# Two-layer hybrid decoder on one core: other dates for the modulation rows, other engines for the first squares

## The chip, the cores and the metric

The kernel runs on one core of one Trainium2 chip. The metric is the time of one execution on the device in microseconds (us); of several executions the median is given. Lower is better. A core has TensorE (matrix products into PSUM), VectorE, ScalarE, GpSimd, and SyncE, which here issues the transfers from HBM into SBUF. The profile calls them PE (PEld for TensorE's weight loads), DVE, ACT, POOL and SP.

## The reference

256 tokens of width 1024 pass through two layers. Each layer is a half-step SwiGLU feed-forward, a token mixer, and a second half-step feed-forward. The mixer of layer 0 is stick-breaking attention, that of layer 1 a gated linear recurrence (RG-LRU). Every sub-layer is normalised and modulated by shift, scale and gate, which come from one conditioning vector c:

```python
c_act = jax.nn.silu(c)
for layer in range(DEPTH):
    mod = (c_act @ mod_w[layer] + mod_b[layer]).reshape(B, N_SUB, 3, D_MODEL)
    h, g = sublayer_input(x, norm_g[layer, 0], mod[:, 0])     # rmsnorm(x) * (1 + scale) + shift, 1 + gate
    x = x + MACARON_W * g * swiglu(h, ffn_w_gu[layer, 0], ffn_w_down[layer, 0])
    h, g = sublayer_input(x, norm_g[layer, 1], mod[:, 1])
    y = stick_breaking_attention(...) if layer == 0 else rglru_block(...)
    x = x + g * y
    h, g = sublayer_input(x, norm_g[layer, 2], mod[:, 2])
    x = x + MACARON_W * g * swiglu(h, ffn_w_gu[layer, 1], ffn_w_down[layer, 1])
return rmsnorm(x, final_norm_g)
```

All is float32. The modulation weights are 2 x 9 x 1024 rows of 1024 numbers, and each layer's 9 x 1024 results are needed before the sub-layer that uses them.

## The kernel before

**Stages.** Six stages follow each other: feed-forward (0, 0), attention, feed-forward (0, 2), feed-forward (1, 0), the recurrent layer, feed-forward (1, 2). Counted as stages they are the first to the sixth; feed-forward (0, 2) is the third and (1, 0) the fourth. The activations x stay in SBUF for the whole program, transposed, as 8 chunks of 128 x 256.

**Products.** To get float32 accuracy from a faster product, each weight block `raw` is split into a high part `wh` (ScalarE, line 520) and a rest `wl` (VectorE, line 523); activations are split the same way into `hx` or `arenar` pairs. One group (line 549) is three products of 128 x 128 by 128 x 256: wh with the high part, wh with the rest, wl with the high part. A feed-forward has an up phase, 22 tiles of 8 x 2 groups that are followed by silu and a multiply, and a down phase of 8 x 22 groups, at the end of each eighth of which a residual is added to x (line 719). In a few places a product is done in plain float32 instead (lines 567, 1151).

**Start of a stage.** The next stage's first up tiles use x times the scale alone (`scaled`, lines 642 to 644; 258 columns, the two more carry the shift). Meanwhile the sums of squares are added over the partitions by a product with ones (line 626), ScalarE turns them into 1/rms (`rms`, `rst`, by Ln and Exp), and `norm_chunk` writes the 8 normalised chunks: a multiply on VectorE (line 652, `hpre`), a split on ScalarE (`hx`) and VectorE (line 656). `hk` is a second copy of one chunk. In the recurrent layer follow the convolutions (lines 1130 and 1133, VectorE), the gates (line 1151, TensorE), and later decays, scans and outputs (lines 1208 to 1224), which the first float32 product of its down phase (line 567) waits for.

**Modulation rows.** A row, in this text, is one block of 128 x 1024 modulation weights, 0.5 MB, which a transfer brings into one of three `rawm` buffers; VectorE multiplies it by silu(c) and sums along it in one instruction (line 582, with a short second record for reading the sum). There are 143 of these, and one row, the first scale row, goes in two halves (line 842). The first 16 belong to the first normalisation: `first_scale` and `early` load them one by one between the first weights. The other 128 are in a list, `todo`. A function made by `hook` is called at every up tile and at every block of the down phase, with a position from 0 to 42; it adds `rate` per step to an account and takes a row off the list for every whole one. At positions from a given one on it takes all that are still missing up to `due`.

**Order of the work.** Nothing is issued in the order in which it is written. Every operation is recorded with an estimated cost, and a list scheduler (`Program.schedule`) puts each engine's instructions into a fixed order, by due times that come from TensorE's order and by the buffers that are free. The estimates (`LAT0`, `RATE`, `c_mm`) are the scheduler's alone: they change the order, and no instruction. At run time each engine, and SP's queue of transfers, works through its list in order and waits at the head. A transfer into a buffer that is still in use holds up all transfers behind it.

**The start.** ScalarE loads the first parameters; SP loads c, x in two halves, two modulation rows, then the first weights. Silu of c, spread over the partitions by TensorE (line 1282), is `cact`, in two halves. The squares of x's chunks are split over ScalarE and VectorE (`square`, line 1290) and added on VectorE (line 1293) into one sum for each half of x. TensorE sums both over the partitions and does eight products that nobody reads (line 1274). Then comes the first normalised chunk, and with it the first real products, 16 in float32 (line 567, `bank<-sg,raw`).

## Time and profile before

| | |
|---|---|
| median of 3 runs | 964.79 us (963.89 to 965.85) |
| the profiled execution, its own time | 967.32 us |
| its span, first to last instruction | 965.6 us |
| granted TensorE clock, mean over the span | 0.998 |
| moved by DMA | 251.25 MB, 260 GB/s over the span |
| DMA engines' busy share, queue of SP | 70.3% |

How to read the profile: times are us from the first instruction. A row of the timeline has start, duration, engine, line of the code, operation, output<-input by the program's names, shapes, and in brackets the idle time ahead with what ended it. A record of TensorE includes the way through its pipeline, so that consecutive products overlap; their pace is read from the starts. A row of the windows has, after the stretch and its length, the busy time of PE, PEld, DVE, ACT and POOL with the number of instructions, the clock, the DMA engines' share and GB/s. With one line picked out, only that line's engine is shown. In the view of waits stand the total, the number of times and the longest.

### The profile page before, as it was taken

To read this page: it belongs to the slowest core of one execution; us is meant where nothing else is said; L and a number is where in the kernel's file an instruction comes from. 1 tells how busy PE (TensorE), PEld (TensorE's weight loads), DVE (VectorE), ACT (ScalarE), POOL (GpSimd) and SP (SyncE) were. 2 spreads that over 40 slices of the span, in tenths; PEclk is the share of its full clock that TensorE was granted. 3 is DMA by queue.
4 is the path that set the end of the run, shared out by engine and by line. 5 is a ranking of instruction groups with operands and counts; after the bars stand their busy time and mean duration, and the time that the engine had idled before them with its cause. 6 is when DMAs were issued, how large, how long until landed. Compare 5 with 4: busy or idle time off the path is not lost.

```text
span 965.6 us, 19759 instructions
## 1 busy us (share of the span) xinstructions
PE 949.1 (98%) x8090; PEld 935.7 (97%) x8090; DVE 799.3 (83%) x1343; ACT 575.6 (60%) x935; POOL 3.8 (0%) x16
## 2 busy tenths in 40 slices
PE   7999999999999999999999999999999999999996
PEld 5999999999999999999999999999899999999996
DVE  6889979999999998888999877799997996555551
ACT  5666555559886765554456444544679785444441
POOL 0000000000000000000000000000000000000000
PEclk9999999999999999999999999999999999999999
DMA  8988989965766599788986877799643746555521
GB/s 296 373 298 319 356 302 344 343 254 212 249 235 207 188 331 359 278 300 299 357 326 238 302 267 292 278 340 349 246 162 134 262 162 238 210 176 209 185 88 44
DMA packets 49341, 251.25 MB, mean 260 GB/s; under 512 B 5601, under 2 KB 6497, under 8 KB 30434
## 3 DMA queue, kind: packets, MB, share of 16 engines
q1 hardware_dynamic: 48530, 249.30, 70.3%
q8 instruction: 63, 1.03, 0.4%
q10 hardware_dynamic: 720, 0.69, 0.2%
q14 instruction: 28, 0.23, 0.1%
HBM read 248.92 MB, written 1.05 MB: 259 GB/s over the span
## 4 chain that ended last, share of the span: by engine, by line
PE 83%; DVE 8%; DMA 5%; ACT 2%; issue 1%; SPq 0%; DVEq 0%; ACTq 0%
PE bank L549 77%; DMA rawm<-in_modw 3%; PE bank L954 2%; DVE wl L523 2%; PE bank L567 1%; DVE rawm L582 1%; DVE arenaf L1133 1%; DMA raw<-in_win 1%; PE bank L1077 1%; ACT arenaf L499 1%; PE bank L1030 1%; PE bank L1055 1%; DMA x<-in_xT 1%; DVE hpre L652 0%; ACT wh L520 0%
## 5 line engine op out<-in xcount | busy, mean ns | idle before, releaser
L549 PE MATMUL bank<-hx,wh 128*128 128x256 f32 (+1 forms) x3204 | 556.7, 278 | 0.4 <-DVE hx L656 0.2
L520 ACT ACTIVATE wh<-raw 128x1024 fp32r<-128x1024 f32 (+1 forms) x332 | 340.7, 1033 | 278.1 <-PE bank L549 172.4
L549 PEld LDWEIGHTS bank<-hx,wh 128*128 128x128 f32 x3204 | 486.7, 188 | 2.0 <-DVE hx L656 0.9
L523 DVE TENSOR_TENSOR wl<-raw,wh 128x1024 fp32r<-128x1024 f32 (+1 forms) x332 | 391.7, 1189 | 103.4 <-ACT wh L520 102.5
L549 PE MATMUL bank<-hx,wl 128*128 128x256 f32 (+1 forms) x1602 | 444.3, 277 | 0.0
L549 PEld LDWEIGHTS bank<-hx,wl 128*128 128x128 f32 x1602 | 301.3, 188 | 0.0
L549 PE MATMUL bank<-arenar,wh 128*128 128x256 f32 x1664 | 284.4, 277 | 0.0
L549 PEld LDWEIGHTS bank<-arenar,wh 128*128 128x128 f32 x1664 | 251.0, 188 | 0.1
L549 PE MATMUL bank<-arenar,wl 128*128 128x256 f32 x832 | 229.7, 276 | 0.0
L582 DVE SCALAR_TENSOR_TENSOR rawm<-rawm,cact 128x1024 f32<-128x1024 f32 x143 | 173.9, 1219 | 17.3 <-DMA rawm<-in_modw 16.9
L549 PEld LDWEIGHTS bank<-arenar,wl 128*128 128x128 f32 x832 | 156.2, 188 | 0.0
L499 ACT ACTIVATE arenar<-a 128x256 fp32r<-128x256 f32 x88 | 35.4, 404 | 3.7 <-DVE a L797 2.4
L719 DVE SCALAR_TENSOR_TENSOR x<-bank,mf,x 128x256 f32<-128x256 f32 x48 | 22.6, 478 | 17.3 <-PE bank L549 17.3
L802 DVE TENSOR_TENSOR arenar<-a,arenar 128x256 fp32r<-128x256 f32 x88 | 36.5, 418 | 0.0
L549 PE MATMUL bank<-hk,wh 128*128 128x256 f32 x156 | 31.1, 290 | 0.5 <-ACT hk L499 0.5
L792 DVE TENSOR_TENSOR a<-bank,sg 128x256 f32<-128x256 f32 x74 | 30.7, 417 | 0.3 <-ACT sg L499 0.3
L499 ACT ACTIVATE hx<-x,mf 128x256 fp32r<-128x256 f32 x40 | 19.7, 504 | 18.7 <-DVE x L719 18.3
L499 ACT ACTIVATE hx<-hpre,mf 128x256 fp32r<-128x256 f32 x48 | 23.5, 502 | 10.9 <-DVE hpre L652 10.8
L499 ACT ACTIVATE sg<-bank 128x256 f32<-128x256 f32 x74 | 27.1, 369 | 3.8 <-PE bank L549 2.9
L499 ACT ACTIVATE sq<-x 128x256 f32<-128x256 f32 x45 | 17.8, 403 | 15.6 <-DVE x L719 15.6
L549 PEld LDWEIGHTS bank<-hk,wh 128*128 128x128 f32 x156 | 24.0, 188 | 1.1 <-ACT hk L499 0.7
L499 ACT ACTIVATE arenaf<-bank 128x384 f32<-128x384 f32 (+1 forms) x45 | 21.4, 525 | 4.8 <-PE bank L1030 1.6
(120 smaller groups left out, 588.4 us busy)
## 6 DMA issues: line engine op xcount, KB each, us to landing
rawm<-in_modw SPq DMA_DIRECT2D x144, 512.0 KB, 6.1
raw<-in_gu SPq DMA_DIRECT2D x72, 1024.0 KB, 5.3
raw<-in_wdn SPq DMA_DIRECT2D x44, 1024.0 KB, 4.8
raw<-in_win SPq DMA_DIRECT2D x10, 1024.0 KB, 7.5
raw<-in_qk SPq DMA_DIRECT2D x8, 1024.0 KB, 6.3
raw<-in_gu SPq DMA_DIRECT2D x13, 512.0 KB, 6.9
raw<-in_gu SPq DMA_DIRECT2D x7, 768.0 KB, 4.2
raw<-in_wout SPq DMA_DIRECT2D x5, 1024.0 KB, 4.9
```

Source lines behind the costliest of these rows:

```text
L499: act.activation(o(), i(), f, **{k: (v() if callable(v) else v) for k, v in kw.items()})
L520: act.activation(h()[:, :m], raw()[:, a : a + m], AF.Copy)
L523: dve.tensor_tensor(lo()[:, :m], raw()[:, a : a + m], f32(h()[:, :m]), ALU.subtract)
L549: pe.matmul(o(b()), wc(u()), xc(v()), start=start and n == 0, stop=stop and n == len(passes) - 1, skip_group_check=True)
L567: pr.op("PE", c_mm(n, 4), lambda: pe.matmul(o(b()), wc(wb()), xc(x32()), start=start, stop=stop, skip_group_check=True), [w, x32] + ([] if ...
L582: dve.scalar_tensor_tensor(raw(), raw(), 1.0, cact(), ALU.mult, ALU.mult, accum_out=m()[:, t : t + 1])
L719: dve.scalar_tensor_tensor(x[d](), acc.b()[:, j * T : (j + 1) * T], gate()[:, d : d + 1], x[d](), ALU.mult, ALU.add)
L792: V(lambda: dve.tensor_tensor(a(), b()[:, T:], sg(), ALU.mult), T, [(b, (1, 0)), sg], [a])
L802: V(lambda: dve.tensor_tensor(y[1](), a(), f32(y[0]()), ALU.subtract), n, [a, y[0]], [y[1]])
L954: pe.matmul(o, u()[:, tb * P : (tb + 1) * P], v()[:, c0 : c0 + 256], start=start and n == 0, stop=k == KD - 1 and n == 2, skip_group_check ...
L1030: pe.matmul(zb[e]()[:, BL[i]], v()[rows, kc], w()[rows, qc], start=False, stop=i == 1 and n == 2, skip_group_check=True)
L1055: pe.matmul(b()[:, :S], ntri, hd(q(), e), start=False, stop=False, skip_group_check=True)
```

## The change

Four things are altered.

1. `rate`: in the third and fourth stage the hook takes 1.3 rows a step in place of 0.9, and its last position is 32 in place of 42. The list is then empty before the fourth stage's down phase has got far.
2. The first scale row and the next three rows (`early` with k below 2) get places in the first stage's float32 arena, which is idle until the first partial sums are stored there, in place of `rawm` buffers. So their transfers do not wait for a `rawm` buffer.
3. At the start the squares are divided anew: of each half of x, the first chunk's square is on VectorE and the other three on ScalarE (before, one more of the second half was on VectorE). VectorE adds them in two pairs, and TensorE sums four blocks over the partitions in place of two.
4. The scheduler's estimates: `LAT0`, the latency of the first transfers, is 2000 in place of 950, and the first sum over the partitions is taken at double cost.

```diff
-LAT0, RATE0, RATE = 950.0, 390.0, 360.0
+LAT0, RATE0, RATE = 2000.0, 390.0, 360.0
...
-    def mod_tile(l, s, w, t, after=(), lat=None, rate=RATE):
+    def mod_tile(l, s, w, t, after=(), lat=None, rate=RATE, raw=None):
 
         m = mraw[l, s, w]
-        raw = Buf(modr)
+        raw = raw or Buf(modr)
...
-            pr.op("PE", c_mm(T, 4), lambda i=i, q=q: pe.matmul(b()[:, :T], ones, q(), start=i == 0, stop=i == len(qs) - 1),
+            pr.op("PE", c_mm(T, 4) * (2 if gen == (0, 0) else 1), lambda i=i, q=q: pe.matmul(b()[:, :T], ones, q(), start=i == 0, stop=i == len(qs) - 1),
...
-                last[:] = [mod_tile(0, 0, w, k, last, LAT0, RATE0)]
+                last[:] = [mod_tile(0, 0, w, k, last, LAT0, RATE0, Buf(F, 8) if k < 2 else None)]
...
-                raw = Buf(modr)
+                raw = Buf(F, 8)
...
-        last[:] = [pr.op("DMA", 450.0, lambda: sp.dma_start(c()[:1, :], cb), [], [c], last, lat=LAT0 - 440.0)]
+        last[:] = [pr.op("DMA", 450.0, lambda: sp.dma_start(c()[:1, :], cb), [], [c], last, lat=510.0)]
...
-            t, q, u, v = Buf(ssqr), Buf(hpr), Buf(sqr), Buf(sqr)
-            for i, (z, eng) in enumerate(((t, "DVE"), (q, "ACT"), (u, "ACT"), (v, "DVE" if d else "ACT"))):
+            t, q, u, v = Buf(ssqr), Buf(hpr), Buf(sqr), Buf(sgr)
+            for i, (z, eng) in enumerate(((t, "DVE"), (q, "ACT"), (u, "ACT"), (v, "ACT"))):
                 square(d + i, z, eng)
-                if i:
-                    add(t, z)
-            total.append(t)
+                if i % 2:
+                    add(*((t, q), (u, v))[i // 2])
+            total += [t, u]
...
-    rate = {0: (1.0, SQ, 42), 1: (1.5, 0, 9), 2: (0.9, 0, 42), 3: (0.9, 0, 42)}
+    rate = {0: (1.0, SQ, 42), 1: (1.5, 0, 9), 2: (1.3, 0, 32), 3: (1.3, 0, 32)}
```

TensorE's order is the same but for the two more sums. Of VectorE's rows at line 582, this many stand in the third stage's up phase, its down phase, the fourth's up phase, its down phase, and behind it: 22, 17, 20, 17 and 4 before; 32, 16, 32, 0 and 0 now (counted between the residuals of line 719).

Two places show what moves. The first is the start. VectorE's order there, before (-) and now (+); ssq and sq hold squares, sg_112 is the one that went to ScalarE, mr and mf are modulation results, arenaf is the arena:

```order
-L1293 TENSOR_TENSOR ssq_99<-ssq_99,sq_96 128x256
-L1290 TENSOR_TENSOR sq_97<-x 128x256
-L1293 TENSOR_TENSOR ssq_99<-ssq_99,sq_97 128x256
-L842 SCALAR_TENSOR_TENSOR rawm_75,mr_154<-rawm_75,cact 128x512
-L582 SCALAR_TENSOR_TENSOR rawm_76,mr_152<-rawm_76,cact 128x1024
-L842 SCALAR_TENSOR_TENSOR rawm_75,mhalf<-rawm_75,cact 128x512
+L1293 TENSOR_TENSOR sq_97<-sq_97,sg_112 128x256
+L842 SCALAR_TENSOR_TENSOR arenaf_204,mr_154<-arenaf_204,cact 128x512
+L842 SCALAR_TENSOR_TENSOR arenaf_204,mhalf<-arenaf_204,cact 128x512
+L582 SCALAR_TENSOR_TENSOR arenaf_204,mr_152<-arenaf_204,cact 128x1024
 L846 SCALAR_TENSOR_TENSOR mr_154<-mr_154,mhalf,pars 128x1
 L848 SCALAR_TENSOR_TENSOR mf_155<-mr_154,pars 128x1
```

A square and two adds fewer stand ahead of the first multiply at line 842, and both halves of the scale row now come ahead of the shift row. ScalarE's order at the same place; hpre, sq and sg take squares, cact the two halves of silu(c):

```order
+L499 ACTIVATE cact<-bank_63 128x512
 L499 ACTIVATE hpre_102<-x 128x256
 L499 ACTIVATE sq_96<-x 128x256
-L499 ACTIVATE sq_97<-x 128x256
+L499 ACTIVATE sg_111<-x 128x256
+L499 ACTIVATE cact<-bank_64 128x512
 L499 ACTIVATE hpre_103<-x 128x256
-L499 ACTIVATE sq_96<-x 128x256
-L499 ACTIVATE cact<-bank_63 128x512
-L499 ACTIVATE cact<-bank_64 128x512
+L499 ACTIVATE sq_97<-x 128x256
+L499 ACTIVATE sg_112<-x 128x256
```

One half of cact moved ahead of all squares, the other between the two halves of x, and a sixth square came in.

The second place is the end of the fourth stage, from the last residual on, where the recurrent layer's normalisation begins (line 652). VectorE before:

```order
L644 SCALAR_TENSOR_TENSOR hx<-x,mf_179,hx 128x256
L619 TENSOR_TENSOR ssq_99<-ssq_99,sq_97 128x256
L582 SCALAR_TENSOR_TENSOR rawm_74,mr_186<-rawm_74,cact 128x1024
L582 SCALAR_TENSOR_TENSOR rawm_76,mr_186<-rawm_76,cact 128x1024
L778 TENSOR_SCALAR bc_105<-bank_64 128x1
L523 TENSOR_TENSOR wl_84<-raw_72,wh_77 128x1024
L778 TENSOR_SCALAR bc_108<-bank_68 128x1
L595 TENSOR_TENSOR mf_183<-mr_182,pars 128x4
L597 TENSOR_TENSOR mr_186<-mr_186,pars 128x4
L603 TENSOR_SCALAR mf_187<-mr_186 128x4
L523 TENSOR_TENSOR wl_85<-raw_71,wh_78 128x1024
L652 SCALAR_TENSOR_TENSOR hpre_103<-x,mf_179,rst_101 128x256
```

and now:

```order
L644 SCALAR_TENSOR_TENSOR hx<-x,mf_179,hx 128x256
L619 TENSOR_TENSOR ssq_99<-ssq_99,sq_97 128x256
L523 TENSOR_TENSOR wl_84<-raw_71,wh_77 128x1024
L778 TENSOR_SCALAR bc_105<-bank_64 128x1
L778 TENSOR_SCALAR bc_108<-bank_68 128x1
L523 TENSOR_TENSOR wl_85<-raw_72,wh_78 128x1024
L652 SCALAR_TENSOR_TENSOR hpre_103<-x,mf_179,rst_101 128x256
```

Two modulation rows and three small steps on their results went from between the last square and the normalisation. SP's queue for the recurrent layer's first weights (in_win), before:

```order
L492 DMA rawm_75<-in_modw 128x1024
L492 DMA rawm_74<-in_modw 128x1024
L492 DMA rawm_76<-in_modw 128x1024
L492 DMA raw_72<-in_win 128x2048
L492 DMA rawm_75<-in_modw 128x1024
L492 DMA rawm_74<-in_modw 128x1024
L492 DMA rawm_76<-in_modw 128x1024
L492 DMA raw_71<-in_win 128x2048
```

and now:

```order
L492 DMA raw_73<-in_wdn 128x2048
L492 DMA raw_71<-in_win 128x2048
L492 DMA raw_72<-in_win 128x2048
L492 DMA raw_73<-in_win 128x2048
L492 DMA raw_71<-in_win 128x2048
L492 DMA raw_72<-in_win 128x2048
L492 DMA raw_73<-in_win 128x2048
```

The weights follow the down phase's own (in_wdn) with no modulation row between them.

## The prediction

> **What bounds the kernel now.** I read the page first, then TensorE's waits, then the chain that ended last, then the timeline at the places where that chain leaves TensorE. The page's first row:
>
> ```profile
> PE 949.1 (98%) x8090; PEld 935.7 (97%) x8090; DVE 799.3 (83%) x1343; ACT 575.6 (60%) x935; POOL 3.8 (0%) x16
> ```
>
> TensorE is occupied in all but 16.5 us of the span. An edit on VectorE, ScalarE or the transfers can win only where TensorE waits for them. The view of waits, TensorE's rows (us in total, times, longest):
>
> ```profile
> PE bank L567 <- ACT sg L499: 1.1, 1, 1.1
> PE bank L567 <- DVE arenaf L1224: 0.8, 1, 0.8
> PE bank L1151 <- DVE arenaf L1133: 0.7, 1, 0.7
> PE bank L549 <- ACT hk L499: 0.5, 1, 0.5
> ```
>
> These are four short waits: one at the start, two at the start of the recurrent layer (L549 for hk, L1151) and one late in it. The chain of waits (start, us, what) gives their places:
>
> ```profile
> 10.12 1.15 DVE rawm L582 x2
> 11.26 0.62 DVE rawm L842 x2
> 12.44 0.50 DVE hpre L652
> 13.02 0.52 ACT sg L499
> 13.58 7.17 PE bank L567 x32
> 20.75 182.13 PE bank L549 x1584
> ...
> 510.00 122.89 PE bank L549 x1080
> ...
> 744.97 0.59 DVE arenaf L1224
> 745.61 7.17 PE bank L567 x32
> ```
>
> Until 13.58 us the chain lies on VectorE and ScalarE; from there TensorE sets the pace, 0.114 us per ordinary product (122.89 / 1080). So the change has three places to gain, A (start), B (start of the recurrent layer), C (its second L567), and much ground on which it must lose nothing.
>
> **A, the start.** The timeline of before (start, us, engine, line; in brackets the idle time ahead and what ended it):
>
> ```profile
> 5.68 0.42 ACT L499 ACTIVATE hpre<-x 128x256 f32<-128x256 f32 x1 [3.19 <-DMA x<-in_xT]
> ...
> 6.01 0.70 ACT L499 ACTIVATE sq<-x 128x256 f32<-128x256 f32 x2
> ...
> 7.61 1.06 ACT L499 ACTIVATE cact<-bank 128x512 f32<-128x512 f32 x2
> ...
> 9.08 0.42 DVE L1293 TENSOR_TENSOR ssq<-ssq,sq 128x256 f32<-128x256 f32 x1
> ...
> 9.43 0.68 DVE L842 SCALAR_TENSOR_TENSOR rawm<-rawm,cact 128x512 f32<-128x512 f32 x1
> ...
> 10.58 1.86 PE L1274 MATMUL bank<-mask,zero 128*128 128x256 bf16 x8
> ...
> 10.88 0.47 ACT L499 ACTIVATE rms<-bank,eps 128x256 f32<-128x256 f32 x1 [0.91 <-PE bank L626]
> ...
> 11.91 0.22 DVE L846 SCALAR_TENSOR_TENSOR mr<-mr,mhalf,pars 128x1 f32<-128x1 f32 x1
> ```
>
> Before, VectorE does nine squares and sums, the last add at 9.08, and L842 follows 0.35 us behind it. The change leaves VectorE six of these, and the last one, sq += sg, waits for ScalarE's sixth square. ScalarE's row from the arrival of x at 5.68 is then six squares of 0.35 (0.70 for two) and one half of cact of 0.53 (1.06 for two); the other half of cact now stands ahead of the squares, in the 3.19 us in which ScalarE waited for x. 6 x 0.35 + 0.53 = 2.63, so the last square ends at about 8.31, its add starts at 8.38, and L842 at 8.38 + 0.35 = 8.73 in place of 9.43. From L842 on VectorE has the same three multiplies (2.48 us from 9.43 to L846 at 11.91), then L846, L848, L652 with 0.53 us from L846 to L652. All of it moves by 0.70 us: L652 from 12.44 to 11.74, L567 from 13.58 to 12.88.
>
> Two things could be late instead. The row's transfer: x was followed in the queue by the first scale row, and this window (us, busy times, clock, share, GB/s)
>
> ```profile
> 6.00:8.00 2.00, 0.19 (x2) 0.10 (x1) 1.86 (x7) 1.73 (x6) 0.00 (x0) 1.00 1.02 416
> ```
>
> shows 416 GB/s, so 0.52 MB takes 1.26 us; x's second half was there by 6.98 at the latest, so I estimate the row at 8.3, and at worst the 9.43 at which L842 found it (gain 0). The other: rstd now waits for four sums on TensorE. Before, rms came 1.38 us behind the end of the last add (9.50 to 10.88); after, 8.80 + 1.38 = 10.2, and 10.9 if the sums queue: at the 0.23 us a pass of the L1274 row, four passes a sum, they take 0.93 each while the adds come some 0.7 apart, so the fourth is up to 0.7 late. With 0.9 for rms and rst that is 11.1 to 11.8, level with L652 at worst. I take 0.70, with ends 0 and 0.9.
>
> Rows in the arena: the third row no longer waits for a rawm buffer, and the fourth not for VectorE's L582, so the queue behind them moves up. TensorE did not wait for those weights after 20.75, so this is cover for A and earns nothing itself. If it were gone, the L549 products would start at their old 20.75, and A would be 0.
>
> **B, the start of the recurrent layer.** TensorE's first two up tiles of 258 columns and one of 256 are the same 144 products here and in the last feed-forward stage. The timeline shows both pieces, and ahead of the waits what the normalisation waited for:
>
> ```profile
> 676.91 0.40 PE L549 MATMUL bank<-hx,wh 128*128 128x258 f32 x2
> ...
> 683.03 0.60 PE L626 MATMUL bank<-ssq,ones 128*128 128x256 f32 x2
> ...
> 684.71 1.06 ACT L520 ACTIVATE wh<-raw 128x1024 fp32r<-128x1024 f32 x1 [1.14 <-DMA raw<-in_win]
> 685.68 0.46 ACT L499 ACTIVATE rms<-bank,eps 128x256 f32<-128x256 f32 x1
> ...
> 687.57 1.27 DVE L652 SCALAR_TENSOR_TENSOR hpre<-x,mf,rst 128x256 f32<-128x256 f32 x3
> ...
> 697.46 0.48 PE L1151 MATMUL bank<-arenaf,rawm 128*128 128x256 f32 x1 [0.66 <-DVE arenaf L1133]
> ...
> 774.53 0.40 PE L549 MATMUL bank<-hx,wh 128*128 128x258 f32 x2
> ...
> 792.06 0.39 PE L549 MATMUL bank<-hx,wh 128*128 128x256 f32 x2
> ```
>
> Here 697.46 - 676.91 = 20.55 us; there 792.06 - 774.53 = 17.53. The surplus, 3.02 us, is what B can give. Its cause: the sums of squares were done at 683.63, but rms stood on ScalarE behind a weight split that waited for its transfer, and that transfer stood in SP's queue behind modulation loads, each of which waits until VectorE has freed a rawm buffer; L652 then came behind a split on VectorE. The rows multiplied in this stretch (count holds two entries for each):
>
> ```profile
> 627.00:677.00 50.00, 19.55 (x32) 1.00 0.93 345
> 677.00:745.00 68.00, 6.04 (x10) 1.00 0.51 187
> ```
>
> That is 16 rows in the down phase and 5 behind it. In the changed order none is left there, and the nine win loads stand together in SP's queue. rms can then follow the sums at about 683.7, L652 at 684.7, almost 3 us earlier: enough for hk and every hx chunk. The 0.66 at L1151 may stay in part, since the convolutions still run on a full VectorE. I take 2.5; ends 0 and 3.0.
>
> **C, the second L567.** It waits 0.8 us for L1224. The work that leads to it (gates, decays, scans) hangs on the gates' products on TensorE, so it moves with B, and on a VectorE that is full until then and loses the modulation rows:
>
> ```profile
> 700.00:720.00 20.00, 20.00 (x160) 19.50 (x160) 19.75 (x40) 14.40 (x29) 0.00 (x0) 1.00 0.41 146
> ```
>
> I take 0.6 of 0.8. The other end is negative: if that work does not move, the wait here grows by all that B gave.
>
> **The up phases, at nothing.** 10 more rows come into the third stage's up phase (22 to 32) and 12 into the fourth's (20 to 32). Rows of the page (busy us, mean ns), of the waits, and one window:
>
> ```profile
> L523 DVE TENSOR_TENSOR wl<-raw,wh 128x1024 fp32r<-128x1024 f32 (+1 forms) x332 | 391.7, 1189 | 103.4 <-ACT wh L520 102.5
> ...
> L582 DVE SCALAR_TENSOR_TENSOR rawm<-rawm,cact 128x1024 f32<-128x1024 f32 x143 | 173.9, 1219 | 17.3 <-DMA rawm<-in_modw 16.9
> ...
> L802 DVE TENSOR_TENSOR arenar<-a,arenar 128x256 fp32r<-128x256 f32 x88 | 36.5, 418 | 0.0
> ```
>
> ```profile
> ACT wh L520 <- PE bank L549: 172.4, 135, 1.7
> ...
> ACT wh L520 <- DMA raw<-in_win: 8.4, 4, 4.2
> ```
>
> ```profile
> 460.00:480.00 20.00, 20.00 (x179) 20.00 (x178) 18.14 (x31) 10.70 (x14) 0.00 (x0) 1.00 0.97 378
> ```
>
> An up tile costs TensorE 48 x 0.114 = 5.47 us. VectorE needs two splits of 1.19, two 256-wide steps of 0.42 (3.22 together), and now 32/22 rows of 1.22: 4.99 us. The transfers bring 1.05 + 0.76 MB in 5.47 us, 331 GB/s, where the window shows 378 with TensorE unbroken. What hides them is the lead: ScalarE's splits mostly wait for TensorE to free a wh buffer, that is, seven halves or some 19 us ahead. Without that lead a tile with two rows would cost VectorE 5.65 us, 0.2 over TensorE's.
>
> A + B + C = 0.7 + 2.5 + 0.6 = 3.8 us. The profiled execution took 967.32 us (965.6 of span), so it would become 963.5; it stands 2.5 above the median of 964.79, which becomes 961.0.
>
> **Rivals.**
>
> *The gain is handed back* (18 in 100). B's earlier start meets the same VectorE: L1151 or L567 waits longer and only A is left: 964.1. For it: the 700 to 720 window, with VectorE full of convolutions and splits. Against: the rows leave just this stretch.
>
> *The clock is not yet full* (5 in 100). The eight L1274 products take 0.23 us each, an ordinary product 0.114: until 12.4 us TensorE ran at half rate. L567 at 13.58 took 7.17 us, as it did at 745.61, so by then the rate was full. L567 now starts 0.7 earlier. If half of it ran at half rate, 7.17 / 2 = 3.6 us would be lost: 964.6. The Trainium skill (TensorE: Matmul & The Clock Gate, Part 1) has the clock half until some 3.4 us of sustained activity, in a free-running window. By that rule, the sums from about 6.8 us on keep TensorE active for longer ahead of L567, which speaks against this rival; a grant one window of 3.4 us late would cost an estimated 1.7. The trace agrees with its two rates; it does not show the window.
>
> *Weights late in the up phases* (7 in 100), the slower side. In SP's queue a weight load now stands more often behind two modulation loads that wait for VectorE. Where the lead is used up, as at a stage's first tiles, the price is that of the win load, 4.2 us. It decides from 1.85 rows a tile ((5.47 - 3.22) / 1.22), against a mean of 1.45. One exposure in each of the two stages is 8.4 - 3.8: 969.4. Against: the lead, and no TensorE wait at 460 to 480.
>
> **How the numbers follow.** The forecast has 70 in 100. Its own range: from 0.7 + 1.5 (half of what B can give) + 0 = 2.2 to 0.9 + 3.0 + 0.8 = 4.7, so 960.1 to 962.6. To leave out no more than 2 in 10 it takes in the handed-back case and 0.5 of measurement: 959.6 to 964.6. About 0.2%, 1.9 us, is what a measurement here can tell from no change; 962.9 is that bound. Faster gets the forecast and 0.04 of the handed-back case, where half of B survives: 0.74. Same gets the rest of it and the clock, 0.14 + 0.05 = 0.19; slower, late weights, 0.07.
>
> **What would show it.** In the new profile: L842 at 8.7, L567 at 12.9; no L582 behind the fourth stage's up phase; L652 some 1 us behind the sums instead of 4; 18.0 us from the first 258-column product to L1151; the wait for L1224 gone. It is wrong if L549 gets waits in the third or fourth stage, or if L1224's wait grows to 3.

## The result, and the profile after

The changed kernel takes 960.58 us in the median of 12 runs (959.54 to 964.37), the kernel before 965.11 (963.35 to 969.81, 12 runs). The ratio is 0.9953, 95% interval 0.9937 to 0.9969: 4.5 us less, 3.0 to 6.1. The forecast was 961.0. The profiled execution took 964.37 us (span 962.7), the one of before 967.32 (965.6): these two stand only 2.95 us apart, and that of the changed kernel is the slowest of its 12 runs. The prediction worked from a profile, so I follow this pair first; the experiments then show what the median has beyond it.

The page's first row and TensorE's waits of the changed kernel:

```profile
PE 949.3 (99%) x8094; PEld 936.8 (97%) x8094; DVE 799.3 (83%) x1340; ACT 577.8 (60%) x936; POOL 3.8 (0%) x16
```

```profile
PE bank L567 <- ACT sg L499: 0.8, 1, 0.8
PE bank L549 <- ACT hk L499: 0.6, 1, 0.6
PE bank L549 <- DVE arenar L802: 0.5, 1, 0.5
```

The waits for L1224 and L1133 are gone. Two L549 waits are new: one for L802, the split's rest of an up tile's result, at the end of the third stage's up phase, and one for hk in the fourth stage. (The wait for hk of before, 0.5 us, was another one, in the recurrent layer at 689.89; it is gone as well.)

**The start.** The chain of waits, then the timeline, of the changed kernel:

```profile
6.73 3.80 PE bank L626 x8
12.71 7.17 PE bank L567 x32
19.88 182.13 PE bank L549 x1584
```

```profile
5.71 0.42 ACT L499 ACTIVATE hpre<-x 128x256 f32<-128x256 f32 x1 [0.47 <-DMA x<-in_xT]
8.51 0.69 DVE L842 SCALAR_TENSOR_TENSOR arenaf<-arenaf,cact 128x512 f32<-128x512 f32 x1
10.61 0.47 ACT L499 ACTIVATE rms<-bank,eps 128x256 f32<-128x256 f32 x1 [1.17 <-PE bank L626]
11.57 0.48 DVE L652 SCALAR_TENSOR_TENSOR hpre<-x,mf,rst 128x256 f32<-128x256 f32 x1 [0.28 <-ACT rst L499]
```

L842 starts at 8.51 (9.43 before) and the first L567 at 12.71 (13.58). L652 waits 0.28 us for rst: what ends last is now the four sums on TensorE (the chain's first row), where it was the modulation rows' multiplies on VectorE.

**The end of the third stage's up phase.** VectorE, then TensorE:

```profile
439.75 1.22 DVE L582 SCALAR_TENSOR_TENSOR rawm<-rawm,cact 128x1024 f32<-128x1024 f32 x1
440.89 0.08 DVE L582 DVE_READ_ACCUMULATOR rawm<-rawm,cact 128x1 f32 x1
440.89 1.22 DVE L523 TENSOR_TENSOR wl<-raw,wh 128x1024 fp32r<-128x1024 f32 x1
442.03 0.42 DVE L802 TENSOR_TENSOR arenar<-a,arenar 128x256 fp32r<-128x256 f32 x1
```

```profile
442.50 0.38 PE L549 MATMUL bank<-arenar,wh 128*128 128x256 f32 x1 [0.50 <-DVE arenar L802]
```

VectorE of before at the same place:

```profile
439.38 1.23 DVE L523 TENSOR_TENSOR wl<-raw,wh 128x1024 fp32r<-128x1024 f32 x1 [1.11 <-ACT wh L520]
440.53 0.42 DVE L802 TENSOR_TENSOR arenar<-a,arenar 128x256 fp32r<-128x256 f32 x1
```

The last up tile's rest is now made behind a row and a weight split, where only a split stood ahead of it, and the down phase needs it at once. From the first 258-column product of the third stage to that of the fourth it is 181.93 us here (313.27 to 495.19) and 181.18 before: 0.75 lost.

**The fourth stage's first tiles.** VectorE, then TensorE:

```profile
500.91 1.22 DVE L582 SCALAR_TENSOR_TENSOR rawm<-rawm,cact 128x1024 f32<-128x1024 f32 x1 [0.66 <-DMA rawm<-in_modw]
502.06 0.08 DVE L582 DVE_READ_ACCUMULATOR rawm<-rawm,cact 128x1 f32 x1
502.06 1.22 DVE L523 TENSOR_TENSOR wl<-raw,wh 128x1024 fp32r<-128x1024 f32 x1
...
505.61 0.48 DVE L652 SCALAR_TENSOR_TENSOR hpre<-x,mf,rst 128x256 f32<-128x256 f32 x1
```

```profile
495.19 0.40 PE L549 MATMUL bank<-hx,wh 128*128 128x258 f32 x2
...
507.94 0.50 PE L549 MATMUL bank<-hk,wh 128*128 128x256 f32 x2 [0.60 <-ACT hk L499]
```

L652 of before:

```profile
504.53 1.27 DVE L652 SCALAR_TENSOR_TENSOR hpre<-x,mf,rst 128x256 f32<-128x256 f32 x3
```

VectorE waits 0.66 us for a row that landed late, so the splits, L652 and hk come late: L652 starts 10.42 us behind the stage's first product, 9.21 before (504.53 - 495.32). The fourth stage takes 182.80 us (181.59 before): 1.21 lost.

**The recurrent layer.**

```profile
677.99 0.40 PE L549 MATMUL bank<-hx,wh 128*128 128x258 f32 x2
...
683.79 0.59 PE L626 MATMUL bank<-ssq,ones 128*128 128x256 f32 x2
...
684.83 0.46 ACT L499 ACTIVATE rms<-bank,eps 128x256 f32<-128x256 f32 x1
...
686.10 1.27 DVE L652 SCALAR_TENSOR_TENSOR hpre<-x,mf,rst 128x256 f32<-128x256 f32 x3
...
695.78 0.92 PE L1151 MATMUL bank<-arenaf,rawm 128*128 128x256 f32 x3
...
771.81 0.40 PE L549 MATMUL bank<-hx,wh 128*128 128x258 f32 x2
```

To L1151 it is 17.79 us (20.55 before), and from there to the last feed-forward stage 76.03 (77.07). Of rows none is left in the stretches from 627 us on (16 and 5 before); the fourth stage's up phase has 30 from 507.3 us on (the count holds two entries for each):

```profile
507.30:627.00 119.70, 36.57 (x60) 1.00 0.89 331
627.00:677.00 50.00, 0.00 (x0) 1.00 0.54 192
677.00:745.00 68.00, 0.00 (x0) 1.00 0.33 125
```

The pair's account: +0.87 at the start, -0.75 and -1.21 in the third and fourth stage, +3.81 in the recurrent layer (2.76 and 1.04, rounded), +0.23 behind it: 2.95, the difference of the spans.

### The profile page after: what moved, and what is told of

The parts are those of the page before. It is cut to its first block, busy times and chain, and to the rows that moved or that the text cites. A ratio compares the mean times of both kernels' runs of the same rounds, so it can differ in the third digit from the quotient of the medians.

```text
span 962.7 us, 19772 instructions
## 1 busy us (share of the span) xinstructions
PE 949.3 (99%) x8094; PEld 936.8 (97%) x8094; DVE 799.3 (83%) x1340; ACT 577.8 (60%) x936; POOL 3.8 (0%) x16
## 4 chain that ended last, share of the span: by engine, by line
PE 77%; DVE 10%; DMA 8%; issue 3%; ACT 2%; DVEq 0%; SPq 0%; ACTq 0%
PE bank L549 69%; DMA rawm<-in_modw 7%; DVE wl L523 4%; DVE rawm L582 3%; PE bank L954 2%; PE bank L567 1%; PE bank L1151 1%; ACT wh L520 1%; DMA raw<-in_gu 1%; PE bank L1077 1%; PE bank L1030 1%; PE bank L626 1%; PE bank L1055 1%; DVE arenar L802 1%; DMA x<-in_xT 0%
## 5 line engine op out<-in xcount | busy, mean ns | idle before, releaser
L549 PE MATMUL bank<-hx,wh 128*128 128x256 f32 (+1 forms) x3204 | 555.7, 278 | 0.3
L549 PEld LDWEIGHTS bank<-hx,wh 128*128 128x128 f32 x3204 | 486.0, 188 | 1.4 <-ACT hx L499 0.3
L549 PE MATMUL bank<-hx,wl 128*128 128x256 f32 (+1 forms) x1602 | 444.2, 277 | 0.0
L549 PEld LDWEIGHTS bank<-hx,wl 128*128 128x128 f32 x1602 | 301.3, 188 | 0.0
L549 PE MATMUL bank<-arenar,wh 128*128 128x256 f32 x1664 | 284.7, 277 | 0.5 <-DVE arenar L802 0.5
L549 PEld LDWEIGHTS bank<-arenar,wh 128*128 128x128 f32 x1664 | 250.8, 188 | 0.8 <-DVE arenar L802 0.7
L549 PE MATMUL bank<-arenar,wl 128*128 128x256 f32 x832 | 229.7, 276 | 0.0
L582 DVE SCALAR_TENSOR_TENSOR rawm<-rawm,cact 128x1024 f32<-128x1024 f32 x140 | 169.9, 1219 | 15.7 <-DMA rawm<-in_modw 15.4
L549 PEld LDWEIGHTS bank<-arenar,wl 128*128 128x128 f32 x832 | 156.2, 188 | 0.0
L499 ACT ACTIVATE arenar<-a 128x256 fp32r<-128x256 f32 x88 | 35.6, 406 | 18.2 <-DVE a L792 15.9
L802 DVE TENSOR_TENSOR arenar<-a,arenar 128x256 fp32r<-128x256 f32 x88 | 36.4, 417 | 0.0
L549 PE MATMUL bank<-hk,wh 128*128 128x256 f32 x156 | 31.1, 290 | 0.6 <-ACT hk L499 0.6
L499 ACT ACTIVATE sq<-x 128x256 f32<-128x256 f32 x44 | 17.5, 404 | 15.6 <-DVE x L719 15.6
L549 PEld LDWEIGHTS bank<-hk,wh 128*128 128x128 f32 x156 | 24.0, 188 | 1.3 <-ACT hk L499 0.8
```

Source lines behind the costliest of these rows:

```text
L499: act.activation(o(), i(), f, **{k: (v() if callable(v) else v) for k, v in kw.items()})
L549: pe.matmul(o(b()), wc(u()), xc(v()), start=start and n == 0, stop=stop and n == len(passes) - 1, skip_group_check=True)
L582: dve.scalar_tensor_tensor(raw(), raw(), 1.0, cact(), ALU.mult, ALU.mult, accum_out=m()[:, t : t + 1])
L802: V(lambda: dve.tensor_tensor(y[1](), a(), f32(y[0]()), ALU.subtract), n, [a, y[0]], [y[1]])
```

## The experiments

The table holds what all profiles gave, in us: from ScalarE's first square of x to the first L567; from there to the second stage of 258-column products (the "first stage" here); the third stage, the fourth and the recurrent layer, each from its first 258-column product to the next stage's; the median, that of the kernel before on the same chip, and the ratio with its interval. The attention took 117.21 us everywhere but in shaped_rephased (118.67, where hx came late once).

| kernel | square to L567 | first | third | fourth | recurrent | median (before) | ratio, 95% |
|---|---|---|---|---|---|---|---|
| before | 7.90 | 183.35 | 181.18 | 181.59 | 97.62 | | |
| changed | 7.00 | 183.34 | 181.93 | 182.80 | 93.81 | 960.58 (965.11) | 0.9953, 0.9937 to 0.9969 |
| start_only | 6.99 | 181.27 | 181.17 | 182.37 | 95.73 | 963.70 (966.63) | 0.9975, 0.9960 to 0.9989 |
| rates_only | 7.89 | 183.34 | 184.34 | 180.96 | 93.81 | 964.50 (966.63) | 0.9975, 0.9962 to 0.9987 |
| start_no_arena | 7.00 | 181.26 | 181.17 | 184.28 | 93.82 | 962.56 (966.63) | 0.9945, 0.9927 to 0.9962 |
| rates_shaped | 7.00 | 181.26 | 181.17 | 180.93 | 93.82 | 962.08 (966.63) | 0.9949, 0.9934 to 0.9964 |
| late_no_multiply | 7.90 | 183.34 | 181.18 | 182.21 | 95.64 | 965.26 (966.52) | 0.9989, 0.9975 to 1.0002 |
| late_no_transfer | 7.90 | 183.34 | 181.22 | 181.38 | 95.83 | 965.81 (966.52) | 0.9989, 0.9972 to 1.0007 |
| old_start_rephased | 7.90 | 181.41 | 181.22 | 180.93 | 96.19 | 965.06 (966.71) | 0.9984, 0.9970 to 0.9998 |
| changed_again | 7.00 | 181.26 | 182.02 | 181.07 | 94.01 | 961.26 (966.71) | 0.9949, 0.9927 to 0.9970 |
| shaped_rephased | 7.00 | 181.82 | 181.18 | 180.93 | 93.82 | 960.69 (966.71) | 0.9943, 0.9927 to 0.9960 |
| late_no_multiply_replanned | 7.89 | 185.59 | 181.17 | 181.98 | 94.33 | 965.22 (966.71) | 0.9979, 0.9960 to 0.9998 |
| old_start_shaped | 7.89 | 183.02 | 181.22 | 180.93 | 93.82 | 964.70 (967.64) | 0.9966, 0.9950 to 0.9983 |
| shaped_rephased_early | 6.99 | 181.41 | 181.18 | 181.15 | 93.82 | 961.08 (967.64) | 0.9936, 0.9922 to 0.9951 |

The runs of one kernel spread over some 5 us, so a profile's stages say more than its total.

**start_only**, the changed kernel with the old rates:

```diff
-    rate = {0: (1.0, SQ, 42), 1: (1.5, 0, 9), 2: (1.3, 0, 32), 3: (1.3, 0, 32)}
+    rate = {0: (1.0, SQ, 42), 1: (1.5, 0, 9), 2: (0.9, 0, 42), 3: (0.9, 0, 42)}
```

> The changed kernel with the rates of rows of the kernel before (0.9 a position in the third and fourth feed-forward stage): the new start alone. Theory (three places, and two small losses that come from the rates): the first L567 at 12.7 us as in the changed kernel (13.58 before), so 0.87 us are won there; they are kept through the third and fourth stage, with no wait for L802 at the end of the third stage's up phase and 18.3 us for the first 144 up products of the fourth stage; the recurrent layer's start (first product of 258 columns to L1151) stays near 20.5 us and L1224's wait near 0.8. In all about 0.9 us less than before, ratio about 0.9991. Rival (the losses come from the earlier start itself, which moves the queue of transfers): the 0.87 us are lost again by the fourth stage, and the time equals the time before.

The start won 0.91 of path, as expected. Three things were not. The recurrent layer's start, up to L1151, took 18.66 us, not 20.5. The fourth stage's first tiles took 18.97 us (492.39 to 511.36) with the old rates too, so that loss is not made by the new ones alone; it is a weak place of both kernels, 17.5 to 20.0 us in the 14 profiles. And the first stage was 2.1 us shorter than before, so the kernel won 2.9 in the median. The chain shows it in one row, with the same number of products as in the changed kernel's third row above:

```profile
19.91 180.06 PE bank L549 x1584
```

**rates_only**, the kernel before with the new rates (the rate line, the other way round):

> The kernel before with only the rates of rows changed (1.3 a position in the third and fourth feed-forward stage). Theory: the first L567 stays at 13.58 us; the recurrent layer's start takes 17.8 us in place of 20.55 (2.76 won), the way from L1151 to the last phase's first product 76.0 in place of 77.1 (1.0 won), and the third and fourth stage lose 0.7 and 1.2 us in the places where the changed kernel lost them (the rest split L802 at the end of the third stage's up phase, the first tiles of the fourth). In all 1.9 us less than before, ratio about 0.998. Rival (the losses are the earlier start's): no loss in the third and fourth stage, 3.8 us less, ratio 0.996. Rival (the recurrent layer's gain needs the start): 20 us there, no gain.

The recurrent layer has its full gain without the new start: 93.81. The fourth stage lost nothing, but the third took 184.34, 3.2 us more than before, with no wait listed there. The windows of TensorE (stretch, busy time, instructions) show why:

```profile
420.00:440.00 20.00, 20.00 (x179) 1.00 0.97 371
446.00:486.00 40.00, 40.00 (x342) 1.00 0.96 357
```

and TensorE's timeline what lies between:

```profile
443.93 0.66 PE L549 MATMUL bank<-arenar,wh 128*128 128x256 f32 x2
444.43 0.28 PE L549 MATMUL bank<-arenar,wl 128*128 128x256 f32 x1
```

Ahead, a product takes 20 / 179 = 0.112 us, behind it 40 / 342 = 0.117. A hesitation of under 0.3 us (two products in 0.50 instead of 0.23) was followed by the slower pace until 513 us; another such stretch went from 332 to 356 us. The hesitation itself stands where the changed kernel waits for L802, and VectorE shows the same order, a row that waits for its transfer, a weight split, then L802:

```profile
441.44 1.23 DVE L582 SCALAR_TENSOR_TENSOR rawm<-rawm,cact 128x1024 f32<-128x1024 f32 x1 [0.74 <-DMA rawm<-in_modw]
443.73 0.42 DVE L802 TENSOR_TENSOR arenar<-a,arenar 128x256 fp32r<-128x256 f32 x1
```

The theory had one of its two places right, but not the size, since most of the loss is the pace behind it; the first rival, which had no losses, failed as well.

**start_no_arena**, rows in rawm again:

```diff
-                last[:] = [mod_tile(0, 0, w, k, last, LAT0, RATE0, Buf(F, 8) if k < 2 else None)]
+                last[:] = [mod_tile(0, 0, w, k, last, LAT0, RATE0)]
...
-                raw = Buf(F, 8)
+                raw = Buf(modr)
```

> The changed kernel, but the first rows go through the three rawm buffers again instead of the idle arena; squares, sums, rates and the first loads' planned latencies stay as changed. Theory (rows in the arena are cover and earn nothing themselves): the first L567 within 0.2 us of 12.7, the first L549 product within 0.2 us of 19.53, TensorE without a wait behind it until the attention; the time is that of the changed kernel within 0.3 us. Rival (the third and fourth row, which then wait for a buffer, hold up the weights in the queue): L567 or the L549 products behind it wait for 0.7 us or more, and the gain at the start is gone: 0.9 us over the changed kernel.

```profile
6.39 0.42 ACT L499 ACTIVATE hpre<-x 128x256 f32<-128x256 f32 x1 [1.23 <-DMA x<-in_xT]
```

```profile
13.39 0.92 PE L567 MATMUL bank<-sg,raw 128*128 128x256 f32 x3 [1.25 <-ACT sg L499]
```

x came 0.7 us later in this execution (6.39 against 5.71; the 14 profiles have 5.7 to 6.4), so L567 stands at 13.39 and not within 0.2 us of 12.7; from x on it is 7.00 us, as with the arena, and TensorE does not wait in the first stage behind it. The arena earns nothing at the start. The fourth stage took 184.28 us here, the longest of all: its first tiles took 20.01 us, with 0.7 of waiting for hk, and the slower pace followed from 511 to 536 us.

**rates_shaped**, the changed kernel with the rows laid out otherwise:

```diff
-    rate = {0: (1.0, SQ, 42), 1: (1.5, 0, 9), 2: (1.3, 0, 32), 3: (1.3, 0, 32)}
-    due = {0: 24, 1: 48, 2: 72, 3: len(todo)}
+    rate = {0: (1.0, SQ, 42), 1: (1.5, 0, 9), 2: (1.3, 0, 42), 3: (1.3, 0, 32)}
+    segs = {2: ((2, 1.3), (19, 0.5), (24, 1.3), (34, 0.5)), 3: ((2, 0.6), (5, 1.5), (24, 1.3))}; due = {0: 24, 1: 48, 2: 72, 3: len(todo)}
...
-            done[0] += r * (pos - done[1] if len(done) > 1 else 1)
+            done[0] += [q for p, q in segs.get(ph, ((0, r),)) if p <= pos][-1] * (pos - done[1] if len(done) > 1 else 1)
```

> The changed kernel with the rows of the third and fourth stage laid out in another way: few (0.5 a position) in the last five tiles of the third stage's up phase and at the end of its down phase, few (0.6) in the first three tiles of the fourth stage, 1.5 a position in the rest of its up phase, the last eight or so in the first half of its down phase. Theory (the two losses are rows that stand ahead of the last rest split and ahead of the fourth stage's first splits): no wait for L802, the first 144 up products of the fourth stage in 18.3 us or less in place of 19.4; the recurrent layer's start stays at 17.8 us. In all 1.5 to 1.9 us less than the changed kernel, about 5.8 less than the kernel before in the median, ratio 0.994. Rival (VectorE at 1.5 rows a tile falls behind TensorE): L549 waits for weights in the fourth stage for over 1 us, and the time is that of the changed kernel or above. Rival (rows in the down phase hold up the recurrent layer): its start takes 19 us or more.

The chain of rates_shaped, then that of rates_only, third and fourth stage:

```profile
317.78 180.73 PE bank L549 x1584
498.94 180.50 PE bank L549 x1584
```

```profile
321.01 183.91 PE bank L549 x1584
505.35 180.52 PE bank L549 x1584
```

Both losses are gone. The total, 4.6 us under before and not 5.8 as expected, cannot be told from that of the changed kernel by the interval.

**late_no_multiply** and **late_no_transfer**, the kernel before with its 21 late rows reduced to 8 columns, in the multiply or in the load. `thin`, a new argument of `mod_tile`, is true in the fourth stage from step 24, in both:

```diff
-                mod_tile(*key, t, after=[pr.last_pe])
+                mod_tile(*key, t, after=[pr.last_pe], thin=ph == 3 and pos >= 24)
```

```diff
-            dve.scalar_tensor_tensor(raw(), raw(), 1.0, cact(), ALU.mult, ALU.mult, accum_out=m()[:, t : t + 1])
+            dve.scalar_tensor_tensor(raw()[:, :8 if thin else D], raw()[:, :8 if thin else D], 1.0, cact()[:, :8 if thin else D], ALU.mult, ALU.mult, accum_out=m()[:, t : t + 1])
```

```diff
-        load_ = dma(raw, modw[l, (s * 3 + w) * KD + t], D, [raw], after, lat, rate)
+        load_ = dma(lambda: raw()[:, :8 if thin else D], modw[l, (s * 3 + w) * KD + t][:, :8 if thin else D], D, [raw], after, lat, rate)
```

> The kernel before, in which the 21 rows that it leaves to the fourth stage's down phase and later are transferred in full but multiplied over 8 of their 1024 columns: their work on VectorE is left out, their transfers and the order stay. Theory of the prediction (the normalisation was late because a weight's transfer stood in the queue behind row loads, and these wait until VectorE has freed a buffer): buffers come free at once, so the queue moves, and the recurrent layer's start (first product of 258 columns to L1151) takes 18 us or a little over in place of 20.55. Rival (it is the transfers' bytes: 10.5 MB more through the queue in this stretch): the start still takes 20 us or more, although VectorE has 25 us less to do.

> The kernel before, in which the same 21 late rows are multiplied in full, but only 8 of their 1024 columns are transferred: 32 bytes a partition instead of 4 KB; the order stays. Theory of the prediction (row loads hold the queue while they wait for VectorE to free a buffer): the loads still wait for the buffers, VectorE still has the multiplies, and the start of the recurrent layer keeps at least half of its surplus, 19 us or more. Rival (the bytes): the weights come earlier, and the start takes 18 us. The wait for L1224, if it goes with the start's surplus, is gone in whichever of the two kernels has the short start.

Both gave 18.56 us from the first product to L1151 and kept both waits (L1133's 0.7 and L1224's 0.8), so they do not tell the two apart, and the theory's 19 us for late_no_transfer failed. The control explains it: with whole rows the start took 20.55, 18.66 and 19.10 us (before, start_only, old_start_rephased). So taking out the work or the transfers is worth 0.1 to 2.0 us, according to which of these three it is set against; and 0.8 us over the 17.78 of the kernels without late rows remains even without the work. VectorE of late_no_multiply shows where:

```profile
681.37 0.08 DVE L582 DVE_READ_ACCUMULATOR rawm<-rawm,cact 128x1 f32 x1
683.78 0.16 DVE L778 TENSOR_SCALAR bc<-bank 128x1 f32<-128x1 f32 x1 [2.32 <-PE bank L549]
683.85 1.22 DVE L523 TENSOR_TENSOR wl<-raw,wh 128x1024 fp32r<-128x1024 f32 x1
...
685.39 1.23 DVE L523 TENSOR_TENSOR wl<-raw,wh 128x1024 fp32r<-128x1024 f32 x1
686.54 0.88 DVE L652 SCALAR_TENSOR_TENSOR hpre<-x,mf,rst 128x256 f32<-128x256 f32 x2
```

VectorE stands idle for 2.32 us at L778, with a weight split behind it that the changed kernel does at 682.06, 4.1 us from its first product, before L778. The order was planned for rows that take time, and VectorE keeps it. Hence **late_no_multiply_replanned**, which is late_no_multiply with a planner that is told that these rows cost next to nothing:

```diff
-        V(fn, D, [raw, cact], [raw, (m, t)])
+        V(fn, 8 if thin else D, [raw, cact], [raw, (m, t)])
```

> As late_no_multiply (the 21 late rows multiplied over 8 columns only, so their work on VectorE is left out), but the planner is told that they cost VectorE next to nothing, so the order of the work around them is planned anew. late_no_multiply kept 95.6 us for the recurrent layer, the waits for L1133 (0.7) and L1224 (0.8) with it, although VectorE was idle for 2.3 us ahead of the normalisation. Theory (these two waits come from the order that was planned around the rows, not from their work): both waits are gone and the recurrent layer takes 93.8 to 94.2 us. Rival (the transfers of the rows, which both kernels keep): 95.6 us again.

L1224's wait is gone, L1133's is down to 0.3, and the layer takes 94.33 in place of 95.64: 1.3 of the 1.8 us to the changed kernel's 93.81 are the order around the rows, not their work (by one profile of each).

**old_start_rephased**: the two paces had come up with start_only and rates_only. The kernel before with one product of zeros:

```diff
-                tiles(accs, k, *weights(gu0[k], k, k >= NA - 1), k == KD - 1)
+                kick_op(accs[0], 0) if k == 1 else None; tiles(accs, k, *weights(gu0[k], k, k >= NA - 1), k == KD - 1)
```

> The kernel before with one product of 64 columns of zeros put among the products of the first feed-forward stage, at about 25 us; everything else as before. It is for a theory that came up with the first runs: in the first stage TensorE goes through some 480 products either at 117.8 or at 113.4 ns each for the whole of it, set by how it restarted behind L567, and the kernels with the old start were found at 117.8 in four profiles of four, those with the new start at 113.4 in three of four; that is worth 2.0 us, and would be the part of the median's gain (4.5 us) that the profile of the changed kernel (2.95) lacks. Theory (the rhythm is decided at a restart and can be broken by an odd product): behind the zeros the products take 113.4 ns, the first stage (first L549 product to the first of 258 columns) 174.9 us or less in place of 176.5, and the median is 1.5 to 2 us under the time before, ratio 0.998. Rival (the rate belongs to something else that lasts through these products, such as the transfers or the operands): 117.8 before and behind it, 176.6 us, no change of the median.

The first stage was 174.59 us from its first L549 product, and the median fell by 1.65, but this profile shows the fast pace ahead of the zeros already: it proves nothing of them, and shows that the old start can have the fast pace too.

**changed_again**, the changed kernel on another chip:

> The changed kernel once more, with a profile on another chip. Theory: the first stage at 113.4 ns a product (174.5 us in place of 176.5), and then a median 4.5 to 5 us under the time before; the recurrent layer 93.8 us again; the wait for L802 at the end of the third stage's up phase, which one of three kernels with these rates showed, and the 1.1 us at the fourth stage's first tiles, which five of seven kernels with either rate showed, may be there or not. Rival (the rate is no property that the new start shifts): 117.8 ns, 176.5 us, and a median 3 us under the time before.

The theory held for the first stage, 174.44 us from its first L549 product; the median fell by 5.5 us, a little more than expected. The third stage was 0.84 over before, again by the slow pace after its first tiles (329 to 352 us).

**shaped_rephased**, both:

> The changed kernel with the rates laid out as in rates_shaped and the product of zeros of old_start_rephased: the version that should be the fastest. Theory: third stage 181.2, fourth 180.9, recurrent layer 93.8 us as in rates_shaped, the first stage at 174.5 us in every run; median 5 to 6 us under the time before, ratio 0.994. Rival (the zeros leave the products at 117.8 ns in some runs): first stage 176.5 us, 3.5 to 4 us under the time before.

Here the zeros, at 31.21 us, came upon the slow pace. TensorE's windows ahead of them and behind:

```profile
20.00:31.00 11.00, 11.00 (x96) 1.00 1.04 404
32.00:52.00 20.00, 20.00 (x179) 1.00 0.99 351
```

11 / 96 = 0.115 us with the entries at its edges (0.118 from start to start), then 0.112. In this profile the slow pace ends at the odd product; six profiles without it had the slow pace until some 56 us behind the first L549 product.

**old_start_shaped**, the old start with the rates of rates_shaped:

> The kernel before with the rates of rates_shaped and nothing else: the effect of rows done early without the accidents that the even rate of 1.3 met. Theory (the even rate wins 1.9 to 3.8 us in the recurrent layer and loses part of it in the third and fourth stage; laid out otherwise it loses none): first product of 258 columns to first product, third stage 181.2, fourth 180.9, recurrent layer 93.8 us (97.6, 95.7 and 96.2 in the three kernels with the old rates and whole rows); from the arrival of x to the first L567 7.57 us as before. In the median 2.5 to 3.5 us under the time before, ratio 0.997. Rival (the recurrent layer needs the even rate's fewer rows in the fourth down phase, or the losses come back): third and fourth stage together over 363 us or the recurrent layer over 94.5, and a median within 1.5 us of the time before.

Third, fourth and recurrent stage as expected, 2.9 us in the median, ratio 0.9966. It also shows what the old start can cost:

```profile
10.89 1.91 PE L1274 MATMUL bank<-mask,zero 128*128 128x256 bf16 x8
```

```profile
13.89 8.78 PE L567 MATMUL bank<-sg,raw 128*128 128x256 f32 x32 [1.09 <-ACT sg L499]
```

The 16 float32 products of L567 (32 records) took 8.78 us instead of 7.17 (9.42 in late_no_multiply_replanned): until 17.2 and 18.2 us by the trace's clock TensorE ran at half rate. In old_start_shaped the starts of these records are 0.427 us apart ahead of 17.2 us and 0.216 behind it.

**shaped_rephased_early**, rates_shaped with the zeros at 20.9 us:

```diff
-                    for g in range(2):
+                    for g in (kick_op(accs[-1], 0) if f == 1 and k == 1 and stop else None, 0, 1)[1:]:
```

> rates_shaped with the product of zeros put three products behind the first L549 product, at about 20 us, in place of 31 us in shaped_rephased: there the products took 117.8 ns ahead of the zeros and 113.4 behind them. Theory (a restart decides the rhythm, and the zeros' restart leads to the fast one): 113.4 ns from 21 us on, first stage 174.5 us; the whole 5 to 6.5 us under the time before in the median, ratio 0.994, with little spread between runs. Rival (the zeros' restart is as open as any other): 117.8 ns behind the zeros, first stage 176.5 us.

First stage 174.59 from its first L549 product, 6.6 us under before, the lowest ratio, and six runs within 1.4 us. In this profile too the pace was fast at the last products ahead of the zeros (0.113 us). Its interval overlaps that of the changed kernel: whether it beats it is open.

## Why the prediction was right, and where not

**A, 0.7 predicted, 0.90 measured** from x to L567, in all seven profiles with the new start. The end that was given as possible (0.9) came about, because L842 moved by 0.92, and the sums, "level with L652 at worst", are what L652 waits for, by 0.28.

**The arena at nothing:** right (start_no_arena).

**B, 2.5 predicted, 2.76 in the pair.** The size is partly luck: with whole rows and the old rates the surplus over 17.78 was 2.77, 0.88 and 1.32 us, and the profile of before was the worst. The mechanism, a transfer behind row loads, is in the profile of before (rms behind a weight split that waited 1.14 us for its transfer), but it carried that scatter at most. Most of the steady part is the order that the planner builds around the rows (late_no_multiply_replanned). The intermediate forecast failed as well: L652 follows the sums' end by 1.72 us (686.10 against 684.38), not by 1, since rms still stands behind a weight split. It was enough: no wait of TensorE followed.

**C, 0.6 predicted, 1.04 measured.** It goes with the order too: the wait stayed in late_no_multiply and went when only the planner's cost was changed.

**The step that failed: "The up phases, at nothing".** The prediction named its sign, L549 waits in the third or fourth stage, and the changed kernel shows two. The lead of seven weight halves did cover the weights; no product of these stages waited for one. But it covers no result that is used at once: the last up tile's rest (L802) and the fourth stage's hk stand in the same VectorE order as the rows and have no lead. Four kernels with the even rate took 364.73, 363.09, 365.45 and 365.30 us for the third and fourth stage, 364.6 in the mean; three with the old rates and whole rows 362.77, 363.54 and 362.15, 362.8; four with the shaped rates 362.2. So in these profiles the even rate gives back 1.8 of the 2.7 us that the recurrent layer wins (96.5 to 93.9 in the mean), and the shaped rates give nothing back.

What the 1.8 us are made of is shown in part only. Most of it is the slower pace: 2.9 us in rates_only, 0.8 in changed_again and, by an estimate of 218 products at 4.4 ns more, 1.0 in start_no_arena, that is 1.2 us in the mean of the four; the other kernels have none of it in these two stages. The hesitations at L802 (changed, rates_only) are the rows' doing by the order on VectorE: no other kernel has one. But the wait for hk comes with the old rates too, and the slow pace of changed_again, like the first one of rates_only, follows a hesitation some 17.2 us into the third stage that all 14 profiles show, mostly without the slow pace behind it. Whether the even rate makes that pace likelier is open.

**What the median has beyond the pair.** The clock rival did not come about, and may be turned round: two of seven profiles with the old start had half rate into L567, none of seven with the new one. And the pace of the first stage was slow in five of seven with the old start and in two of seven with the new one; both profiles of the pair are among the slow ones, so the pair could not show this. Without the kernels with zeros, the first stage is 183.7 in the mean with the old start and 181.7 with the new: 2.0 us, about what start_only won beyond its 0.9. Adding up means, 0.9 + 2.0 + 2.7 - 1.8 = 3.8, within the measured 3.0 to 6.1. Of the 2.0, some 1.3 us are the pace (slow in five of six against one of five, 2.07 us each) and 0.6 the clock (1.61 and 2.25 us over six). Seven against seven profiles do not settle that the new start shifts these odds; the median of start_only supports it.

So the forecast of 961.0 came out in part by luck, by two errors of opposite sign: losses in the up phases that it put at nothing, and gains in TensorE's pace and clock in the first stage that it did not know of.

## What to carry to other kernels

A lead in weights hides work on a shared engine only from the products that wait for weights: look for results that are made and used at once at a phase's edges, and keep added work away from there. Work that a planner places can cost more than its own time: take its cost out of the plan as well as out of the kernel before saying what it is worth. And where runs scatter by more than the effect, compare stages over several profiles; a single pair can hold a stage's best and worst.

## What the runs showed of the hardware

**Two paces of one product.** A stream of 256-column fp32r products, each with its weight load, ran at 0.113 or 0.118 us from start to start at full granted clock, and not by the program alone: the first stage of the same kernel took 183.34 us in the profile of the changed kernel and 181.27 in changed_again. The pace is taken up within a few products of a restart and kept. In the feed-forward stages the profiles hold eleven slow stretches. One ended at the zeros; nine lasted 23 to 56 us and one, across the change from the third to the fourth stage, 69; these ten ended without any hesitation (no start more than 0.13 us behind the last), each where the products go from reading hk to reading hx, though not every such change ended one. Why a restart takes the one or the other pace stayed open. It is worth 2.07 us over the first stage, and in rates_only a hesitation of under 0.3 us was followed by a slow stretch that cost about 2 us by the end of the stage.

**The clock's grant falls on steps.** By the trace's clock the full rate lasted 938.7, 942.1, 945.5 or 948.9 us in the 14 profiles, steps of 3.41, and began between 11.0 and 18.2 us. (These are the start and length of the clock's records in the traces. There is no record from ahead of that start, and the clock column of the windows reads 1.00 there although the products ran at half rate.) With the new start TensorE works from 6.7 us to the end of the L1274 products without a break; with the old one, the sums stand 0.44 us apart, begin 1.2 us later, and two executions of seven were granted it so much later that L567 lost 1.6 and 2.25 us: 9.0 and 10.3 us behind the start of the first sum, against 3.8 to 5.6 in the other 12 profiles. Whether the break is the cause is not shown. The Trainium skill (TensorE: Matmul & The Clock Gate, Part 1) has the clock released after a window of about 3.4 us of activity that runs free of the kernel, so that one kernel's cold products vary from run to run. The traces agree with both: the steps are of 3.41 us, and before and late_no_multiply_replanned, whose TensorE rows are alike until 10.57 us, got the full rate at 12.26 and 18.16 us.
